# Attention scores as fp32 matmuls on the two row halves of the array, with unsplit q and k

## The chip, the cores and the metric

The kernel runs on one core of one Trainium2 chip. The metric is the device time of one execution in microseconds (us). A core has a matrix engine (PE, TensorE), a vector engine (DVE), an activation engine (ACT), a general engine (POOL, GpSimd) and a queue engine (SP) that issues the transfers (DMA). Matmuls write to PSUM, which has eight banks of 512 fp32 numbers per partition; everything else lives in SBUF, over 128 partitions.

## The reference, cut to what matters

Two layers of a hybrid encoder over 256 tokens, width 1024. Each layer normalises its input, applies one wide input projection, and feeds three branches: forgetting attention (16 heads of 64), a state-space scan, and differential attention (8 heads, each with two score matrices of 64 dims). The scores of the first and of the third are what the change touches:

```python
for i in range(L // Q_BLOCK):                                   # forgetting attention, Q_BLOCK = 128
    s = jnp.einsum('bhqd,bhkd->bhqk', q[:, :, q0:q1], k[:, :, :q1]).astype(jnp.float32) * scale
    s = s + F[:, :, q0:q1, None] - F[:, :, None, :q1]           # F: cumulative log forget gate
    p = jax.nn.softmax(jnp.where(tk <= tq, s, -jnp.inf), axis=-1).astype(v.dtype)
    outs.append(jnp.einsum('bhqk,bhkd->bhqd', p, v[:, :, :q1]))
...
for i in range(L // Q_BLOCK):                                   # differential attention, c = 0, 1
    s = jnp.einsum('bhcqd,bhckd->bhcqk', q[:, :, :, q0:q1], k[:, :, :, :q1]).astype(jnp.float32) * scale
    p = jax.nn.softmax(jnp.where(ck <= cq, s, -jnp.inf), axis=-1)
    a = (p[:, :, 0] - lam * p[:, :, 1]).astype(v.dtype)
    outs.append(jnp.einsum('bhqk,bhkd->bhqd', a, v[:, :, :q1]))
```

All inputs and outputs are fp32.

## The kernel before

**The projections.** Weights come from memory in units of 128x1024 (`raw`), and are split into a rounded part and a rest (`whi`, ACT, L231; `wlo`, DVE, L232) of the type fp32r, so that a product of three fp32r matmuls (hi·hi, hi·lo, lo·hi) has fp32 precision. `bform` (L249, 128x512 outputs) makes projections with tokens on the partitions, `aform` (L264, 128x256 outputs) makes those with features on the partitions. Together they are the main stream of PE work, in the order of `plan`. Everything else is written as generators (jobs); `pump` steps them between two projections, and the framework's scheduler then sets the final order on each engine by its own estimate of times. An engine works through its own list in that order.

**Scores before.** q and k have their features on the partitions: a tile of 128 partitions holds two heads (or the two halves of one differential head), one in partitions 0 to 63 and one in 64 to 127. `split_qk` builds from each tile new fp32r tiles: `stack_q` (L380, L381) puts the rounded half and its rest one above the other in 128 partitions, `stack_k` (L385 to L388) the rounded k twice, and its rest twice. `scores` then makes, for one head and one PSUM bank, four matmuls over all 128 rows of the array: 128 keys for the first 128 tokens and 256 keys for the next 128, each with k (L400) and with its rest (L401). DVE adds the bias and takes the maximum (L403), ACT takes the exponential (L406).

**The mask of forgetting attention.** `small_chain` makes the gates on DVE and then their running sums by matmuls (L359 to L366); DVE copies them out (`sc_cum`, L368, L369), SP writes them to memory (`scr`, L371) and reads them back spread over the partitions into the tile `sc` of each pair of heads (L422, L423); POOL masks two blocks of `sc` (L426). DVE's L403 reads `sc` as bias and writes the scores over it. Behind the softmax `sc` is transposed (L447) and multiplied by the values into `po` (L457), each head of a pair on one half of the array's columns.

**PSUM.** Three banks `pp` for the projections, three `pq` for scores, transposes of weights of attention and part of the scan, two `pt` for the other transposes, the scan's states and the products with the values.

Of the kernel before, what the change touches and what calls it, by code (L numbers as in the profile page):

```python
# [11 lines left out]
F32 = mybir.dt.float32  # L12
F32R = mybir.dt.float32r
AF = mybir.ActivationFunctionType
# [3 lines left out]
P = 128  # L18
# [78 lines left out]
def trunk(ctx: ExitStack, tc: tile.TileContext, x, norm_w, weights, small, vectors,  # L97
# [10 lines left out]
    sm = ctx.enter_context(tc.tile_pool(name="sm", bufs=2))  # L108
    dr = ctx.enter_context(tc.tile_pool(name="dr", bufs=1, space=bass.MemoryType.DRAM))
    pp = ctx.enter_context(tc.tile_pool(name="pp", bufs=3, space=bass.MemoryType.PSUM))  # L110
    pq = ctx.enter_context(tc.tile_pool(name="pq", bufs=3, space=bass.MemoryType.PSUM))
    pt = ctx.enter_context(tc.tile_pool(name="pt", bufs=2, space=bass.MemoryType.PSUM))

    SMALL = nc.sync

# [12 lines left out]
    def bank(pool, name):  # L128
        return pool.tile([P, 512], F32, name=name)
# [63 lines left out]
                                   op0=ALU.mult, op1=ALU.subtract)  # L193

    def split_rows(src, hi, lo, tt, c):
        ps = bank(pt, "pt")
        for j in range(4):
            PE.transpose(ps[:, j * P:(j + 1) * P], src[:, j * P:(j + 1) * P], ident)  # L198
        ts = slice(tt * P, (tt + 1) * P)
        p4 = ps.rearrange("p (i j t) -> p i j t", i=2, t=P)  # L200
        for i in range(2):
            last = split_bank(p4[:, i], hi[2 * c + i][:, :, ts], lo[2 * c + i][:, :, ts])
        return last
# [169 lines left out]

    SPANS = ((0, slice(0, P)), (1, slice(P, 384)))

    LOH, HIH = slice(0, 64), slice(64, P)

    def stack_q(src, dst):
        for q, main, rest in zip(dst, (LOH, HIH), (HIH, LOH)):
            S.copy(out=q[main], in_=src[main])  # L380
            V.tensor_tensor(out=q[rest], in0=src[main], in1=q[main].bitcast(F32), op=ALU.subtract)  # L381

    def stack_k(src, dst):
        for k, kl, main, rest in zip(dst[0:2], dst[2:4], (LOH, HIH), (HIH, LOH)):
            S.copy(out=k[main], in_=src[main])  # L385
            V.tensor_tensor(out=kl[main], in0=src[main], in1=k[main].bitcast(F32), op=ALU.subtract)
            S.copy(out=k[rest], in_=src[main])
            S.copy(out=kl[rest], in_=kl[main].bitcast(F32))  # L388

    def split_qk(key, src):  # L390
        tiles = [a2(dtype=F32R) for _ in range(2 if key[1] == "q" else 4)]
        (stack_q if key[1] == "q" else stack_k)(src, tiles)
        return tiles

    def scores(st, pre, b, i, sc, bias, nm, rs):
        j, tk = b % 2, st[f"{pre}k{b // 2}"]
        q, k, kl = st[f"{pre}q{b // 2}"][i], tk[i], tk[2 + i]
        ps = bank(pq, "pq")
        for o, qs, n in ((0, slice(0, P), P), (P, slice(P, T), T)):
            PE.matmul(ps[:, o:o + n], lhsT=q[:, j, qs], rhs=k[:, j, 0:n], start=True, stop=False)  # L400
            PE.matmul(ps[:, o:o + n], lhsT=q[:, j, qs], rhs=kl[:, j, 0:n], start=False, stop=True)  # L401
        for t, sl in SPANS:
            V.tensor_tensor_reduce(out=sc[:, sl], in0=ps[:, sl], in1=bias[:, sl], scale=-0.125, scalar=BIG,  # L403
                                   op0=ALU.add, op1=ALU.min, accum_out=nm[:, t:t + 1])
        for t, sl in SPANS:
            S.activation(out=sc[:, sl], in_=sc[:, sl], func=AF.Exp, scale=-1.0,  # L406
                         bias=nm[:, t:t + 1], accum_out=rs[:, t:t + 1])

    def fox(l):
        st = L[l]  # L410
# [5 lines left out]
    def fox_pair(l, b, yhi, ylo):  # L416
        st = L[l]
        hb, j = b // 2, b % 2
        yield from need(l, "scr")
        sc = sp.tile([P, 2, 384], F32, name="sc")  # L420
        rows = st["scr"][2 * b:2 * b + 2, :]
        SMALL.dma_start(sc[:, :, 0:P], rows[:, 0:P].partition_broadcast(P))  # L422
        SMALL.dma_start(sc[:, :, P:384], rows.partition_broadcast(P))  # L423
        for i in (0, 2):
            v = sc[:, :, i * P:(i + 1) * P]
            G.affine_select(out=v, in_=v, pattern=[[0, 2], [-1, P]], compare_op=ALU.is_ge,  # L426
                            fill=NEG, base=0, channel_multiplier=1)
        yield 1, 0.0
        yield from need(l, f"fq{hb}", f"fk{hb}")
        nm = sm.tile([P, 2, 2], F32, name="nm")  # L430
        rs = sm.tile([P, 2, 2], F32, name="rs")
        for i in range(2):
            scores(st, "f", b, i, sc[:, i, :], sc[:, i, :], nm[:, i, :], rs[:, i, :])
        ri = sm.tile([P, 2, 2], F32, name="ri")
        V.reciprocal(out=ri, in_=rs)
        V.tensor_scalar(out=ri, in0=ri, scalar1=0.5, scalar2=None, op0=ALU.mult)
        for i in range(2):
            for t, sl in SPANS:
                V.tensor_scalar(out=sc[:, i, sl], in0=sc[:, i, sl], scalar1=ri[:, i, t:t + 1],
                                scalar2=None, op0=ALU.mult)  # L440
        yield 2, 2.2
        yield from need(l, "fv", f"fg{hb}")
        pTs = []
        for i in range(2):
            ps = bank(pq, "pq")
            for t in range(3):
                PE.transpose(ps[:, t * P:(t + 1) * P], sc[:, i, t * P:(t + 1) * P], ident)  # L447
            pT = tp.tile([P, 384], F32, name="pT", bufs=3)
            done = S.copy(out=pT, in_=ps[:, 0:384]).ins
            pTs.append(pT)  # L450
        yield 1, 0.0
        po = bank(pt, "pt")
        with tc.high_priority(URGENT):
            for t, o, n in ((0, 0, T), (1, P, P)):
                for i in range(2):
                    h = 2 * b + i
                    mm = PE.matmul(po[64 * i:64 * i + 64, o:T],  # L457
                                   lhsT=st["fv"][t][h // 8][:, h % 8 * 64:(h % 8 + 1) * 64],
                                   rhs=pTs[i][:, t * T:t * T + n], start=(t == 0), stop=(t == 1))
                    if t + i == 0:  # L460
                        tc.add_manual_dep(mm.ins, done.name, mybir.DependencyInfo(
                            mybir.DependencyClass.Sync, mybir.DependencyReason.DATA), reason="both heads")
        yt = sc[:, 0, 0:T]
        V.tensor_tensor(out=yt, in0=po[:, 0:T], in1=st[f"fg{hb}"][:, j, :], op=ALU.mult)
        S.copy(out=at(yhi, b), in_=yt)
        V.tensor_tensor(out=at(ylo, b), in0=yt, in1=at(yhi, b).bitcast(F32), op=ALU.subtract)
        st["_yA"][1] += 1
        if st["_yA"][1] == 8:
            st["yA"] = st["_yA"][0]
        yield 1, 0.75  # L470
# [21 lines left out]
    def ssd_cb(l):  # L492
# [5 lines left out]
        for gp in range(2):  # L498
# [7 lines left out]
            V.tensor_tensor(out=m, in0=ps.rearrange("p (a b) -> p a b", b=P),  # L506
                            in1=upper.unsqueeze(1).broadcast_to([P, 4, P]), op=ALU.mult)
            cb.append(m)
        ps = bank(pt, "pt")
        for g in range(4):  # L510
            PE.transpose(ps[:, g * P:(g + 1) * P], bT[g // 2][:, g % 2, 0:P], ident)
        btok = sm.tile([P, 512], F32, name="btok", bufs=1)
# [6 lines left out]
    def ssd_x(l, c, tt):  # L519
# [7 lines left out]
        xdt, y = a2([P, 512]), a2([P, 512])  # L527
        st[f"xdt{tt}"].append(xdt)
        st[f"ys{tt}"].append(y)
        ps = bank(pt, "pt")  # L530
        for j in range(4):
            PE.transpose(ps[:, j * P:(j + 1) * P], xc[j // 2][:, j % 2, tt * P:(tt + 1) * P], ident)  # L532
        p3 = ps.rearrange("p (h d) -> p h d", d=64)
# [9 lines left out]
    def ssd_group(l, g):  # L543
# [33 lines left out]
                                   in1=st["cb"][c][:, 2 * (g % 2):2 * (g % 2) + 2, :].rearrange("p b k -> p (b k)")  # L577
                                   .unsqueeze(1).broadcast_to([P, 2, 256]), op=ALU.mult).ins
        yield 2, 3.2
        ps = bank(pt, "pt")  # L580
        PE.matmul(ps[:, 0:256], lhsT=st["btok"][:, g * P:(g + 1) * P], rhs=xdd[:, gs], start=True, stop=True)
        S.copy(out=st0[:, gs], in_=ps[:, 0:256])
        ps = bank(pq, "pq")
# [45 lines left out]
    def transposed(l, name, y, scale):  # L629
        yield 1  # L630
        yhi, ylo = halves()
        for j2 in range(4):
            ps = bank(pt, "pt")
            for i in range(2):
                j = 2 * j2 + i
                for tt in range(2):
                    PE.transpose(ps[:, i * T + tt * P:i * T + (tt + 1) * P], y[tt][j // 4][:, j % 4 * P:(j % 4 + 1) * P], ident)  # L637
            for i in range(2):
                j = 2 * j2 + i
                split_bank(ps[:, i * T:(i + 1) * T], at(yhi, j), at(ylo, j), scale(j))  # L640
            if j2 == 3:
                L[l][name] = (yhi, ylo)
            if j2 % 2:
                yield (1, 1.6)
# [3 lines left out]
    def rope(l, c):  # L648
# [16 lines left out]
        V.tensor_tensor(out=rp, in0=rp, in1=sw, op=ALU.add)  # L665
        for d_, s_ in views:
            SMALL.dma_start(s_, d_)
        yield 1, 2.4
        for key, src in (("dq", q), ("dk", k)):
            for jj in range(2):  # L670
                st[f"{key}{2 * c + jj}"] = split_qk(key, src[jj])
            yield 1, 1.2 if key[1] == "k" else 2.4

    def diff(l):
        L[l]["_d"] = 0
# [3 lines left out]
    def diff_head(l, h):  # L679
        st, pr = L[l], par[l]  # L680
        yield from need(l, f"dq{h // 2}", f"dk{h // 2}")
        sc = sp.tile([P, 2, 384], F32, name="sc")
        nm = sm.tile([P, 2, 2], F32, name="dnm")
        rs = sm.tile([P, 2, 2], F32, name="drs")
        for i in range(2):
            scores(st, "d", h, i, sc[:, i, :], bmask, nm[:, i, :], rs[:, i, :])
        ri = sm.tile([P, 2, 2], F32, name="dri")
        V.reciprocal(out=ri, in_=rs)
        V.tensor_scalar(out=ri[:, 1, :], in0=ri[:, 1, :], scalar1=pr["nlam"], scalar2=None, op0=ALU.mult)
# [37 lines left out]
    def plan(l):  # L727
# [38 lines left out]

        def t_evac(key):
            def f(jj, ps):
                st[f"{key[0:2]}{2 * int(key[2]) + jj}"] = split_qk(key, ps.rearrange("p (a t) -> p a t", t=T))
            return f  # L770

        def r_evac(key):
# [257 lines left out]
```

## Time and profile before

| | |
|---|---|
| time, median of 3 runs | 944.5 us (944.32 to 945.57) |
| profiled execution | 943.72 us, span of its instructions 942.0 us |
| PE busy | 928.9 us (99%), 6052 matmuls |
| DVE busy | 698.9 us (74%) |
| ACT busy | 598.0 us (63%) |
| POOL busy | 40.4 us (4%) |
| granted TensorE clock, mean | 0.994 |

Busy times are a share of the span. A matmul's record is longer than the room it takes in the stream, since the next one starts before it ends; the chain of work (which counts from one end to the next) is the view that gives a matmul's price in a full stream. An fp32 matmul has two records in the trace, an fp32r matmul one.

### The profile page before, as it was taken

How to read it: one execution, taken by the hardware profiler on the slowest of the kernel's cores; microseconds unless marked ns; L12 is line 12 of the kernel's file. 1: busy time of each engine (PE TensorE's matmuls, PEld its weight loads, DVE VectorE, ACT ScalarE, POOL GpSimd, SP SyncE). 2: the span in 40 equal slices, each digit the busy share in tenths (PEclk: the TensorE clock that was granted, in tenths of full speed). 3: DMA queues.
4: the chain of work that ended last, by engine and by line, in shares of the span. 5: the costliest groups of instructions: out<-in, count | busy, mean ns of one | idle time of the engine just before them, and what ended most of it. 6: DMA issues, size and time to landing. Idle time of an engine off the chain costs nothing.

```text
span 942.0 us, 16514 instructions
## 1 busy us (share of the span) xinstructions
PE 928.9 (99%) x6052; PEld 831.3 (88%) x6052; DVE 698.9 (74%) x1434; ACT 598.0 (63%) x1141; POOL 40.4 (4%) x71
## 2 busy tenths in 40 slices
PE   7999999999999999999999999999999999999997
PEld 6999999988898988888889999998889899888885
DVE  5778788989667877765758778789877677787473
ACT  5678786644567868554546869666545696885442
POOL 1002200000000000100000110000000000010000
PEclk7999999999999999999999999999999999999999
DMA  6866634674555655555558674456646456555551
GB/s 237 272 216 195 213 116 153 216 224 144 180 199 160 187 191 157 177 173 190 188 173 270 212 213 140 132 179 209 202 153 206 145 186 190 189 169 167 182 175 45
DMA packets 60320, 172.47 MB, mean 183 GB/s; under 512 B 7312, under 2 KB 15824, under 8 KB 60240
## 3 DMA queue, kind: packets, MB, share of 16 engines
q1 hardware_dynamic: 60240, 171.43, 55.8%
q8 instruction: 47, 0.77, 0.4%
q14 instruction: 33, 0.27, 0.1%
HBM read 167.14 MB, written 2.16 MB: 180 GB/s over the span
## 4 chain that ended last, share of the span: by engine, by line
PE 96%; DMA 2%; DVE 1%; ACT 0%; issue 0%; SPq 0%; POOL 0%; POOLq 0%
PE pp L249 51%; PE pp L264 33%; PE pq L400 2%; PE pq L401 1%; PE pt L457 1%; PE pq L447 1%; PE pq L590 1%; DMA raw<-in_weights_dram 1%; PE pt L637 1%; PE pt L198 1%; PE pq L702 1%; PE pq L600 0%; PE pt L532 0%; PE pt L710 0%; PE pq L503 0%; PE pt L709 0%
## 5 line engine op out<-in xcount | busy, mean ns | idle before, releaser
L249 PE MATMUL pp<-whi,a 128*128 128x512 f32 (+1 forms) x1472 | 451.6, 386 | 1.2 <-ACT whi L231 0.8
L232 DVE TENSOR_TENSOR wlo<-raw,whi 128x1024 fp32r<-128x1024 f32 (+1 forms) x296 | 349.6, 1193 | 79.4 <-ACT whi L231 76.3
L231 ACT CAST whi<-raw 128x1024 fp32r<-128x1024 f32 (+1 forms) x296 | 301.9, 1028 | 116.5 <-PE pp L249 68.3
L264 PE MATMUL pp<-a,whi 128*128 128x256 f32 x1792 | 332.4, 285 | 0.0
L249 PEld LDWEIGHTS pp<-whi,a 128*128 128x128 f32 x1472 | 272.9, 189 | 55.1 <-ACT whi L231 1.5
L264 PEld LDWEIGHTS pp<-a,whi 128*128 128x128 f32 x1792 | 281.2, 191 | 1.3 <-issue 1.0
L249 PE MATMUL pp<-wlo,a 128*128 128x512 f32 (+1 forms) x736 | 280.9, 384 | 0.0
L264 PE MATMUL pp<-a,wlo 128*128 128x256 f32 x896 | 254.4, 284 | 0.0
L264 PEld LDWEIGHTS pp<-a,wlo 128*128 128x128 f32 x896 | 171.5, 191 | 0.8 <-issue 0.8
L249 PEld LDWEIGHTS pp<-wlo,a 128*128 128x128 f32 x736 | 138.5, 189 | 25.8 <-DVE wlo L232 0.5
L183 POOL TENSOR_TENSOR rstd<-rstd,mhalf 128x2 f32<-128x2 f32 (+2 forms) x26 | 18.9, 727 | 740.0 <-DVE rstd L181 719.1
L477 DVE SCALAR_TENSOR_TENSOR a<-sw,pT,a 128x255 f32<-128x255 f32 (+2 forms) x96 | 42.0, 477 | 6.1 <-ACT a L474 6.0
L406 ACT ACTIVATE sc<-sc,dnm 128x128 f32<-128x128 f32 x64 | 28.6, 450 | 8.4 <-DVE dnm L403 8.3
L400 PE MATMUL pq<-a,a 128*128 128x128 f32 (+1 forms) x128 | 31.9, 284 | 0.4 <-DVE nm L403 0.4
L188 ACT CAST a<-pt 128x256 fp32r<-128x256 f32 x32 | 11.5, 371 | 32.6 <-PE pt L198 26.5
L819 DVE SCALAR_TENSOR_TENSOR a<-a,pp 128x512 f32<-128x512 f32 x24 | 16.4, 682 | 20.4 <-PE pp L249 20.4
L401 PE MATMUL pq<-a,a 128*128 128x128 f32 (+1 forms) x128 | 31.5, 269 | 0.0
L406 ACT ACTIVATE sc<-sc,nm 128x128 f32<-128x128 f32 (+1 forms) x64 | 28.5, 447 | 2.1 <-DVE nm L403 2.0
L426 POOL TENSOR_SCALAR_AFFINE_SELECT sc<-sc 128x256 f32<-128x256 f32 x32 | 19.7, 619 | 156.6 <-DMA sc<-scr 138.1
L400 PEld LDWEIGHTS pq<-a,a 128*128 128x128 f32 x128 | 23.7, 191 | 0.9 <-DVE nm L403 0.6
L403 DVE CUSTOM_DVE_ANT_0 sc<-pq,sc 128x128 f32<-128x128 f32 (+1 forms) x64 | 19.5, 351 | 6.6 <-POOL sc L426 5.6
L401 PEld LDWEIGHTS pq<-a,a 128*128 128x128 f32 x128 | 23.6, 191 | 0.3
(159 smaller groups left out, 807.7 us busy)
## 6 DMA issues: line engine op xcount, KB each, us to landing
raw<-in_weights_dram SPq DMA_DIRECT2D x280, 512.0 KB, 4.4
raw<-in_weights_dram SPq DMA_DIRECT2D x16, 272.0 KB, 3.3
sc<-scr SPq DMA_DIRECT2D x16, 256.0 KB, 5.5
a<-scr SPq DMA_DIRECT2D x16, 256.0 KB, 6.2
a<-in_x_dram SPq DMA_DIRECT2D x8, 256.0 KB, 5.3
sc<-scr SPq DMA_DIRECT2D x16, 128.0 KB, 5.0
a<-in_norm_w_dram SPq DMA_DIRECT2D x4, 256.0 KB, 6.5
rp<-a SPq DMA_DIRECT2D x32, 32.0 KB, 4.0
```

The costliest lines, as they stand in the source:

```text
L183: G.tensor_tensor(out=r[:, 0:width], in0=r[:, 0:width], in1=mhalf[:, 0:width], op=ALU.pow)
L231: S.copy(out=hi, in_=raw)
L232: V.tensor_tensor(out=lo, in0=raw, in1=hi.bitcast(F32), op=ALU.subtract)
L249: PE.matmul(ps[:, 0:n], lhsT=at(a, kt)[:, ts], rhs=w[:, k, 0:n], start=((u, k, i) == order[0]), stop=((u, k, i) == order[-1]))
L264: PE.matmul(ps[:, j * T:(j + 1) * T], lhsT=w[:, k, c0:c0 + P], rhs=at(a, kt), start=(kt == 0 and j == 0 and i == 0), stop=(kt == KT - 1 an ...
L400: PE.matmul(ps[:, o:o + n], lhsT=q[:, j, qs], rhs=k[:, j, 0:n], start=True, stop=False)
L401: PE.matmul(ps[:, o:o + n], lhsT=q[:, j, qs], rhs=kl[:, j, 0:n], start=False, stop=True)
L403: V.tensor_tensor_reduce(out=sc[:, sl], in0=ps[:, sl], in1=bias[:, sl], scale=-0.125, scalar=BIG, op0=ALU.add, op1=ALU.min, accum_out=nm[: ...
L406: S.activation(out=sc[:, sl], in_=sc[:, sl], func=AF.Exp, scale=-1.0, bias=nm[:, t:t + 1], accum_out=rs[:, t:t + 1])
L426: G.affine_select(out=v, in_=v, pattern=[[0, 2], [-1, P]], compare_op=ALU.is_ge, fill=NEG, base=0, channel_multiplier=1)
L477: V.scalar_tensor_tensor(out=xc[:, s:T], in0=u[:, 0:T - s], scalar=pr["conv"](j, k), in1=xc[:, s:T], op0=ALU.mult, op1=ALU.add)
L819: V.scalar_tensor_tensor(out=t, in0=t, scalar=1.0, in1=ps, op0=ALU.add, op1=ALU.mult)
```

## The change

Scores are made from q and k as they come out of the projection (for differential attention as `rope` leaves them), in fp32. The splitting functions are gone; `t_evac` copies a projection's bank to one fp32 tile. `scores` now takes both heads of a pair (or both halves of a differential head) and two banks: for 128 and for 256 keys it issues one matmul with partitions 0 to 63 of q and k and one with partitions 64 to 127, which lie on the upper and lower 64 rows of the array. The first of the four also waits for `held`, the instruction on POOL that last wrote `sc`: the second L426 of the pair for forgetting attention, a new one-column memset for differential attention. Four banks are `pq` and one is `pt`; all but the products with the values use `pq`. Some of `rope`'s yields change.

```diff
-    pq = ctx.enter_context(tc.tile_pool(name="pq", bufs=3, space=bass.MemoryType.PSUM))
-    pt = ctx.enter_context(tc.tile_pool(name="pt", bufs=2, space=bass.MemoryType.PSUM))
+    pq = ctx.enter_context(tc.tile_pool(name="pq", bufs=4, space=bass.MemoryType.PSUM))
+    pt = ctx.enter_context(tc.tile_pool(name="pt", bufs=1, space=bass.MemoryType.PSUM))
...
-    def stack_q(src, dst):
...
-    def stack_k(src, dst):
...
-    def split_qk(key, src):
...
-    def scores(st, pre, b, i, sc, bias, nm, rs):
-        j, tk = b % 2, st[f"{pre}k{b // 2}"]
-        q, k, kl = st[f"{pre}q{b // 2}"][i], tk[i], tk[2 + i]
-        ps = bank(pq, "pq")
+    def scores(st, pre, b, sc, bias, nm, rs, held):
+        j, q, k = b % 2, st[f"{pre}q{b // 2}"], st[f"{pre}k{b // 2}"]
+        ps = [bank(pq, "pq") for _ in range(2)]
         for o, qs, n in ((0, slice(0, P), P), (P, slice(P, T), T)):
-            PE.matmul(ps[:, o:o + n], lhsT=q[:, j, qs], rhs=k[:, j, 0:n], start=True, stop=False)
-            PE.matmul(ps[:, o:o + n], lhsT=q[:, j, qs], rhs=kl[:, j, 0:n], start=False, stop=True)
...
+            for i in range(2):
+                r = slice(64 * i, 64 * i + 64)
+                mm = PE.matmul(ps[i][:, o:o + n], lhsT=q[r, j, qs], rhs=k[r, j, 0:n], start=True, stop=True)
+                if o + i == 0:
+                    tc.add_manual_dep(mm.ins, held.name, mybir.DependencyInfo(
+                        mybir.DependencyClass.Sync, mybir.DependencyReason.DATA), reason="place for the scores")
...
-            G.affine_select(out=v, in_=v, pattern=[[0, 2], [-1, P]], compare_op=ALU.is_ge,
-                            fill=NEG, base=0, channel_multiplier=1)
+            held = G.affine_select(out=v, in_=v, pattern=[[0, 2], [-1, P]], compare_op=ALU.is_ge,
+                                   fill=NEG, base=0, channel_multiplier=1).ins
...
+        held = G.memset(sc[:, 0, 0:1], 0.0).ins
...
-                st[f"{key[0:2]}{2 * int(key[2]) + jj}"] = split_qk(key, ps.rearrange("p (a t) -> p a t", t=T))
+                t = a2()
+                S.copy(out=t, in_=ps.rearrange("p (a t) -> p a t", t=T))
+                st[f"{key[0:2]}{2 * int(key[2]) + jj}"] = t
```

The order moves with it. On PE in the first layer, from the last sum of the gates (L366) on, the kernel before goes on with 19 projection matmuls and the first scores (`a_615` is a q tile, `a_835` and `a_837` are k and its rest; the other L264 rows of this stretch read like the ones shown):

```order
L366 MATMUL pq<-ones,sc_l 16x128
L264 MATMUL pp<-a_150,wlo 128x256
...
L264 MATMUL pp<-a_151,wlo 128x256
L400 MATMUL pq<-a_835,a_615 128x128
L264 MATMUL pp<-a_152,whi 128x256
L264 MATMUL pp<-a_156,whi 128x256
L264 MATMUL pp<-a_152,wlo 128x256
L264 MATMUL pp<-a_152,whi 128x256
L401 MATMUL pq<-a_837,a_615 128x128
L400 MATMUL pq<-a_835,a_615 128x256
L401 MATMUL pq<-a_837,a_615 128x256
```

In the changed kernel 65 projection matmuls stand between L366 and the first scores (L382; `a2_827` is k, `a2_615` q, `pq_831` and `pq_832` are the banks of the two heads):

```order
L264 MATMUL pp_996<-a2_150,whi_550 128x256
L382 MATMUL pq_831<-a2_827,a2_615 128x128
L382 MATMUL pq_832<-a2_827,a2_615 128x128
L382 MATMUL pq_831<-a2_827,a2_615 128x256
L382 MATMUL pq_832<-a2_827,a2_615 128x256
```

So the first scores moved 46 projection matmuls further from L366, and the four of a pair stand together. The sums L359 to L366 themselves moved ahead by 21 projection matmuls. Two projection matmuls later the second pair follows, twelve later the third, and the fourth another two later; the third and fourth stand like this (`pq_928` and `pq_929` are the third pair's banks, `pq_951` and `pq_952` the fourth's):

```order
L382 MATMUL pq_928<-a2_924,a2_666 128x128
L382 MATMUL pq_928<-a2_924,a2_666 128x256
L382 MATMUL pq_929<-a2_924,a2_666 128x128
L382 MATMUL pq_929<-a2_924,a2_666 128x256
...
L382 MATMUL pq_951<-a2_924,a2_666 128x128
L382 MATMUL pq_951<-a2_924,a2_666 128x256
...
L382 MATMUL pq_952<-a2_924,a2_666 128x128
L382 MATMUL pq_952<-a2_924,a2_666 128x256
```

In these two pairs one head's matmuls stand ahead of the other's, and in the fourth a projection matmul stands between the heads. Elsewhere a pair's rows alternate between the heads, as in the fence before, except that in the last differential head of a layer one matmul stands apart. Per layer the 16 pairs stand in 14 uninterrupted stretches. The second layer has the same order.

On DVE, the copies of the running sums to SBUF stood like this before, in the first layer (L386 is one of the splits of k):

```order
L362 COPY sc_acs<-pq 128x32
L232 TENSOR_TENSOR wlo<-raw,whi 128x1024
L368 COPY sc_cum<-pq 32x256
L386 TENSOR_TENSOR a_838<-pp,a_836 64x512
L369 TENSOR_SCALAR sc_cum<-sc_cum 16x256
```

and stand like this in the changed kernel:

```order
L362 COPY sc_acs<-pq 128x32
L368 COPY sc_cum<-pq 32x256
L369 TENSOR_SCALAR sc_cum<-sc_cum 16x256
L232 TENSOR_TENSOR wlo<-raw,whi 128x1024
```

Nothing stands between the copies any more.

## Rows read from the trace of the kernel before

**Rows 1.** The page, part 1: busy us, share of the span, instructions.

```profile
PE 928.9 (99%) x6052; PEld 831.3 (88%) x6052; DVE 698.9 (74%) x1434; ACT 598.0 (63%) x1141; POOL 40.4 (4%) x71
```

**Rows 2.** Who PE waited for: us in total, times, longest us.

```profile
PE pt L198 <- DVE a L210: 2.6, 1, 2.6
PE pq L940 <- POOL mhalf L147: 2.0, 1, 2.0
PE pp L249 <- ACT whi L231: 0.8, 1, 0.8
PE pq L400 <- DVE nm L403: 0.4, 1, 0.4
```

**Rows 3.** The chain from 71.9 us: start us, us, what; one head's scores.

```profile
71.94 0.06 PE pq L400
...
72.40 0.60 PE pp L264 x5
```

**Rows 4.** The chain, 160 to 210 us: fp32 matmuls of 128 and 256 columns.

```profile
160.42 0.89 PE pq L503 x8
...
209.27 0.86 PE pt L581 x4
```

**Rows 5.** The chain from 86 us: products with the values, on column halves.

```profile
86.52 0.33 PE pq L447 x3
86.85 0.80 PE pt L457 x8
87.65 0.81 PE pq L447 x6
...
94.37 0.80 PE pt L457 x8
95.17 3.06 PE pp L264 x24
```

**Rows 6.** The chain from 59.9 us, in the first layer: last sum, projections.

```profile
59.98 0.22 PE pq L366 x2
60.20 2.46 PE pp L264 x19
```

**Rows 7.** DVE from 60 us, in order of time: start us, us, line.

```profile
60.70 0.41 DVE L368 COPY sc_cum<-pq 32x256 f32<-32x256 f32 x1
61.25 0.69 DVE L386 TENSOR_TENSOR a<-pp,a 64x512 fp32r<-64x512 f32 x1
61.97 0.28 DVE L369 TENSOR_SCALAR sc_cum<-sc_cum 16x256 f32<-16x256 f32 x1
```

**Rows 8.** POOL from 68 us, in order of time; idle before it in brackets.

```profile
69.60 0.41 POOL L426 TENSOR_SCALAR_AFFINE_SELECT sc<-sc 128x256 f32<-128x256 f32 x1 [0.28 <-DMA sc<-scr]
...
71.26 0.89 POOL L426 TENSOR_SCALAR_AFFINE_SELECT sc<-sc 128x256 f32<-128x256 f32 x2 [0.34 <-DMA sc<-scr]
```

**Rows 9.** The chain from 519 us, in the second layer: the mask's way.

```profile
519.81 0.22 PE pq L366 x2
...
522.12 3.54 DMA scr<-sc_cum
...
525.72 3.57 DMA sc<-scr
...
530.80 0.41 POOL sc L426
```

**Rows 10.** Groups by line on ACT and DVE: count, busy us, mean ns, idle before.

```profile
L388 ACT CAST a<-a 64x512 fp32r<-64x512 f32 x32 | 19.8, 619 | 0.6
L381 DVE TENSOR_TENSOR a<-pp,a 64x512 fp32r<-64x512 f32 x16 | 11.0, 689 | 0.9 <-ACT a L380 0.4
L403 DVE CUSTOM_DVE_ANT_0 sc<-pq,sc 128x128 f32<-128x128 f32 (+1 forms) x64 | 19.5, 351 | 6.6 <-POOL sc L426 5.6 <-PE pq L401 0.6
L464 DVE TENSOR_TENSOR sc<-pt,a 128x256 f32<-128x256 f32 x16 | 6.8, 422 | 7.5 <-PE pt L457 7.2
```

More of the change, by code (lines that the diff above doesn't have):

```diff
@@ L195, in split_rows @@
     def split_rows(src, hi, lo, tt, c):
-        ps = bank(pt, "pt")
+        ps = bank(pq, "pq")
         for j in range(4):
@@ L374, in trunk @@
     SPANS = ((0, slice(0, P)), (1, slice(P, 384)))
-    LOH, HIH = slice(0, 64), slice(64, P)
-    def stack_q(src, dst):
-        for q, main, rest in zip(dst, (LOH, HIH), (HIH, LOH)):
-            S.copy(out=q[main], in_=src[main])
-            V.tensor_tensor(out=q[rest], in0=src[main], in1=q[main].bitcast(F32), op=ALU.subtract)
-    def stack_k(src, dst):
[L384 to L388, printed above, removed]
@@ L390, in split_qk @@
-    def split_qk(key, src):
-        tiles = [a2(dtype=F32R) for _ in range(2 if key[1] == "q" else 4)]
-        (stack_q if key[1] == "q" else stack_k)(src, tiles)
-        return tiles
-    def scores(st, pre, b, i, sc, bias, nm, rs):
-        j, tk = b % 2, st[f"{pre}k{b // 2}"]
-        q, k, kl = st[f"{pre}q{b // 2}"][i], tk[i], tk[2 + i]
-        ps = bank(pq, "pq")
-        for o, qs, n in ((0, slice(0, P), P), (P, slice(P, T), T)):
-            PE.matmul(ps[:, o:o + n], lhsT=q[:, j, qs], rhs=k[:, j, 0:n], start=True, stop=False)
-            PE.matmul(ps[:, o:o + n], lhsT=q[:, j, qs], rhs=kl[:, j, 0:n], start=False, stop=True)
[L402 to L407, printed above, removed]
+    def scores(st, pre, b, sc, bias, nm, rs, held):
+        j, q, k = b % 2, st[f"{pre}q{b // 2}"], st[f"{pre}k{b // 2}"]
+        ps = [bank(pq, "pq") for _ in range(2)]
+        for o, qs, n in ((0, slice(0, P), P), (P, slice(P, T), T)):
+            for i in range(2):
[4 more added lines that the diff above has]
+                        mybir.DependencyClass.Sync, mybir.DependencyReason.DATA), reason="place for the scores")
+        for i in range(2):
+            for t, sl in SPANS:
+                V.tensor_tensor_reduce(out=sc[:, i, sl], in0=ps[i][:, sl], in1=bias(i)[:, sl], scale=-0.125,
+                                       scalar=BIG, op0=ALU.add, op1=ALU.min, accum_out=nm[:, i, t:t + 1])
+            for t, sl in SPANS:
+                S.activation(out=sc[:, i, sl], in_=sc[:, i, sl], func=AF.Exp, scale=-1.0,
+                             bias=nm[:, i, t:t + 1], accum_out=rs[:, i, t:t + 1])
@@ L431, in fox_pair @@
         rs = sm.tile([P, 2, 2], F32, name="rs")
-        for i in range(2):
-            scores(st, "f", b, i, sc[:, i, :], sc[:, i, :], nm[:, i, :], rs[:, i, :])
+        scores(st, "f", b, sc, lambda i: sc[:, i, :], nm, rs, held)
         ri = sm.tile([P, 2, 2], F32, name="ri")
@@ L508, in ssd_cb @@
             cb.append(m)
-        ps = bank(pt, "pt")
+        ps = bank(pq, "pq")
         for g in range(4):
@@ L529, in ssd_x @@
         st[f"ys{tt}"].append(y)
-        ps = bank(pt, "pt")
+        ps = bank(pq, "pq")
         for j in range(4):
@@ L579, in ssd_group @@
         yield 2, 3.2
-        ps = bank(pt, "pt")
+        ps = bank(pq, "pq")
         PE.matmul(ps[:, 0:256], lhsT=st["btok"][:, g * P:(g + 1) * P], rhs=xdd[:, gs], start=True, stop=True)
@@ L632, in transposed @@
         for j2 in range(4):
-            ps = bank(pt, "pt")
+            ps = bank(pq, "pq")
             for i in range(2):
@@ L667, in rope @@
             SMALL.dma_start(s_, d_)
-        yield 1, 2.4
+        yield 2, 2.4
         for key, src in (("dq", q), ("dk", k)):
             for jj in range(2):
-                st[f"{key}{2 * c + jj}"] = split_qk(key, src[jj])
-            yield 1, 1.2 if key[1] == "k" else 2.4
+                st[f"{key}{2 * c + jj}"] = src[jj]
+        yield 1, 0.0
     def diff(l):
@@ L682, in diff_head @@
         sc = sp.tile([P, 2, 384], F32, name="sc")
+        held = G.memset(sc[:, 0, 0:1], 0.0).ins
         nm = sm.tile([P, 2, 2], F32, name="dnm")
         rs = sm.tile([P, 2, 2], F32, name="drs")
-        for i in range(2):
-            scores(st, "d", h, i, sc[:, i, :], bmask, nm[:, i, :], rs[:, i, :])
+        scores(st, "d", h, sc, lambda i: bmask, nm, rs, held)
         ri = sm.tile([P, 2, 2], F32, name="dri")
```

## The prediction, made before the changed kernel had run

> **What bounds the kernel now.** I read the page's busy shares first: PE is busy 99% of the span [rows 1]. Since a busy PE may still wait inside a record, the list of whom PE waited for comes next: 2.6, 2.0 and 0.8 us belong to the start (first transposes, warm-up, first weights), and in the hundreds of us behind it there is one wait of 0.4 us, at the scores [rows 2]. So PE's stream is the bound, and the price of an edit is what it does to that stream, read from the chain of work, which counts from one end to the next. What ACT and DVE save is worth nothing unless PE waits for it later: the change takes some 128 casts of about 0.62 us off ACT and 64 subtractions of about 0.69 us off DVE [rows 10], 79 and 44 us, and gives ACT 16 copies; but PE waits for neither. That work is covered by the stream of projections.
>
> **What the scores cost before.** One head runs from 71.94 to 72.40 us: 0.46 us [rows 3]. 64 heads (16 per layer and branch): 29.4 us.
>
> **What they cost in fp32.** An fp32 matmul has two records. Of 128 columns, eight records take 0.89 us, 0.11 us each; of 256 columns, four take 0.86 us, 0.215 us each [rows 4]. A pair of heads now has four records of each size, 1.30 us if they run one after another on the array. The trace has no matmul on row halves. The nearest is L457, on column halves, with just these eight records: its piece takes 0.80 us [rows 5]. That is 0.65 us for two halves at the same time, plus 0.15. The bounds of a pair's stream are therefore 0.65 and 1.30 us; I take 0.65, as the form nearest by count, type and size does it: 32 x 0.65 = 20.8 us.
>
> **What changing the array's form costs.** The 0.15 us ahead of L457 is one side. Behind it, six transposes take 0.81 us where three take 0.33 us, so 0.15 more; 24 projection matmuls take 3.06 us, where 0.60 us for five [rows 3] would give 2.88, so 0.18 more [rows 5]. In and out is about 0.31 us. It falls on each uninterrupted stretch of scores, of which the new order has 14 per layer: 28 x 0.31 = 8.7 us. The bounds are 0 (row halves might switch freely) and 8.7; I take 8.7, since the only measured switch paid it both ways.
>
> **Where halves don't stand side by side.** In the third and fourth pair of each layer one head stands ahead of the other. The fourth has a projection matmul between them and loses the whole overlap, 0.65 us; the third lies between 0 and 0.44 us lost (one record of 0.215 can still overlap at the seam), I take 0.22; the last differential head has its two 256-column matmuls apart, 0.43. That is 1.3 us per layer, 2.6 in all; bounds 1.0 and 3.0, the lower if PE looks past a whole head.
>
> So the scores go from 29.4 to 20.8 + 8.7 + 2.6 = 32.1 us: **+2.7 us**.
>
> **The wait for the mask.** Before, L403 on DVE waited for POOL's mask (5.6 us in all [rows 10]), while PE went on. Now the first score matmul of a pair waits itself, and behind it on PE stands everything, projections above all. How late is the mask? In the first layer L366 ends at 60.20 us [rows 6], the first pair's second mask ends at 70.01 us [rows 8]: 9.8 us. In the second layer it is 520.03 to 531.21 us, 11.2 us; the write to memory takes 3.54 us there and the read 3.57 us and more [rows 9]. What the change shortens is DVE's part: L369 ended at 62.25 us, 2.05 us behind L366 [rows 6, 7], with a 0.69 us subtraction and the end of a weight split in between. With L368 (0.41) and L369 (0.28) alone it would be 0.8 us, so the mask comes 1.25 us sooner: 8.55 and 9.95 us behind L366. PE has 65 projection matmuls for that, 65 x 0.12 = 7.8 us. It waits 0.75 us in the first layer and 2.15 us in the second. In the first layer the second pair's mask ends 1.66 us behind the first's (71.67 against 70.01 [rows 8]); PE comes to it after a pair (0.65), the switch (0.31) and two projection matmuls (0.24), 1.2 us, and waits 0.45 us more. Together **3.35 us**. The bounds: nothing, if both transfers together land 2.15 us faster than they did in the second layer; 6.15 us, if they are slower in each layer by another 1.4 us, by which the layers differ. I take the measured latencies. The 0.4 us that PE waited before at L400 [rows 2] goes.
>
> **What costs nothing.** That L359 comes 21 projection matmuls earlier (2.5 us) is paid for by the four subtractions that left DVE's queue ahead of it (4 x 0.69 = 2.8 us). The third pair needs the first's banks back: DVE takes four L403 for that, 1.4 us [rows 10], and PE is 2.4 us away. The single bank `pt` is asked for again after 24 projection matmuls at least, 2.9 us, and freed in the first branch by one 0.42 us instruction [rows 10]; if the longer release in the third branch is late, each time costs some tenths, for which the range has room. SP's queue keeps its order but for two weight loads that now stand behind the ten mask reads; their units are needed some 20 us later. The new memsets on POOL (4% busy [rows 1]) wait for a free `sc`, as DVE did.
>
> **The sum.** +2.7 + 3.35 - 0.4 = +5.65 us. On the profiled execution's 943.72 us (span 942.0) it gives 949.4 us; on the median of the runs, 0.8 us above it, **950.1 us**.
>
> [...] The column halves of L457 take 0.80 us for what is 1.30 us in a row [rows 5, 4]; two records that follow each other in the program on one half have let those of the other half pass. [...]
>
> **The rivals.**
> 1. *The row halves run one after another.* A pair costs 1.30 us. For: no row of the trace shows row halves together. Against: the column halves. 32 pairs take 41.6 us, against 20.8 + 2.6: 950.1 + 18.2 = 968 us. Chance 0.10.
> 2. *Strict order with overlap at the seams only.* A record of one half then overlaps only the last one of the other half ahead of it. For a pair that is 0.11 + 0.11 + 0.11 + 0.105 + 0.215 + 0.215 = 0.865 us, 27.7 us for 32 pairs, and 1.3 us more for the heads that stand apart: 29.0 against 23.4, +5.6 and 955.7 us. Against: the same order would give L457 1.0 us, and it took 0.80. Chance 0.08.
> 3. *Row halves switch without the 0.31 us* (ends on the faster side). [...] It makes the kernel faster by over 0.2% (about what a measurement of this kernel can tell from no change; 1.9 us) once 0.27 of the 0.31 us is gone at each stretch, the waits for the mask staying. For: the measured switch is one of columns. Against: both of its sides paid, also the one back to the full array. Chance 0.11.
> 4. *The masks come in time.* The scheduler put 65 matmuls there by its own estimate; if the transfers land by 2 us sooner now that fewer weight loads stand among them, the 3.35 us goes: 946.8 us, and 945.2 if the heads that stand apart cost 1.0 and not 2.6 us. Against: the mask was late for L403 in both layers. Chance 0.13, a little over half of it within 0.2%.
>
> **How the numbers follow.** My forecast has 0.58; its own range, from the bounds of the mask (0 to 6.15) and of the order (1.0 to 3.0), is 945 to 953.5 us. A range of 942 to 957.5 us leaves out the first rival (0.10) and most of the third (0.09). Faster: the third rival and a little of the fourth, 0.13. Within 0.2% (942.6 to 946.4): most of the fourth and the low end of the forecast, 0.12. Slower: 0.75.
>
> **What would show it.** In the chain after, a stretch of one pair (eight records of L382) of 0.80 us, one of two pairs of 1.45, and the projection piece behind it 0.15 to 0.18 us over 0.12 us a matmul; 1.45 us for one pair would be the first rival, 1.0 the second, 0.65 the third. In the list of PE's waits a new line, PE at L382 for POOL's mask, of 2.5 to 4 us in about three times, the largest in the second layer; without it the fourth rival is right. ACT should be some 70 us and DVE some 40 us less busy, with PE's count of records unchanged at 6052. The prediction is wrong if PE waits at other places, above all for the single bank `pt` or for a memset on POOL.

## The result, and the profile after

| | before | after |
|---|---|---|
| median of 5 runs | 944.5 us (943.86 to 945.57) | 953.13 us (952.68 to 953.57) |
| profiled execution, span | 943.72, 942.0 us | 952.68, 950.6 us |
| mean granted TensorE clock | 0.994 | 0.997 |

The ratio is 1.0092, with a 95% interval of 1.0082 to 1.0103: slower by 8.6 us, where 5.6 were forecast.

The page after, part 1 (compare [rows 1]):

```profile
PE 932.2 (98%) x6052; PEld 819.1 (86%) x6052; DVE 660.4 (69%) x1370; ACT 532.0 (56%) x1029; POOL 41.3 (4%) x87
```

ACT is 66 us less busy and DVE 38.5, with the same 6052 records on PE. None of the 104 us shows in the time, because PE's stream is still the bound. Whom PE waited for (us in total, times, longest), against [rows 2]:

```profile
PE pq L198 <- DVE a L210: 3.2, 2, 2.5
PE pp L249 <- ACT a L748: 2.1, 2, 1.1
PE pq L926 <- POOL mhalf L147: 2.0, 1, 2.0
PE pp L249 <- ACT a L188: 1.9, 2, 1.2
PE pq L382 <- POOL sc L411: 1.3, 2, 1.0
PE pp L249 <- ACT whi L231: 0.8, 1, 0.8
```

L198, L926, L188 and L231 belong to the first 25 us; L188 had 0.4 us before. Behind the start two waits are new. One was forecast, L382 for the mask. The other was not: the projections (L249) for L748, the tanh that copies a finished mixing-gate projection out of its bank.

The chain of work in the first layer, from the second pair of scores on (start us, us, what; compare [rows 3]):

```profile
68.08 0.93 PE pq L382 x8
69.01 1.63 PE pp L264 x12
70.64 0.86 PE pq L382 x8
71.50 0.43 PE pp L264 x2
71.93 0.85 PE pq L382 x4
72.78 0.32 PE pp L264
73.09 0.85 PE pq L382 x4
73.94 2.34 PE pp L264 x18
...
108.92 1.51 PE pq L382 x16
110.43 1.63 PE pp L264 x12
```

Read the pieces against each other. A stretch of two pairs (x16) takes 1.51 us and one of a single pair (x8) 0.86. The second pair adds 0.65 us, which is the price that the prediction gave to two halves side by side, and 0.86 - 0.65 = 0.21 us is the way in. Behind a stretch 12 projections take 1.63 us where 12 x 0.12 = 1.44 would do, and two take 0.43 for 0.24: 0.19 us is the way out. In the trace the records of the stretch at 108.9 us start in twos, 7 ns apart. The third pair (70.64), whose heads stand one after the other, costs 0.86 us like the others; its four records of 128 columns start first, in twos 13 to 14 ns apart, and then its four of 256 (70.57 to 70.79 us, then 70.89 to 71.12), though in the program one head's 256 columns stand ahead of the other's 128. The fourth, with a projection between its heads, costs 0.85 twice: one head alone takes as long as a pair.

The mask's way in the second layer (compare [rows 9]):

```profile
522.21 0.42 DVE sc_cum L368
...
522.66 0.29 DVE sc_cum L369
...
522.97 1.65 DMA scr<-sc_cum
...
524.68 3.59 DMA sc<-scr
...
528.42 1.28 POOL sc L411
...
530.10 1.04 POOL sc L411
...
531.19 0.93 PE pq L382 x8
```

DVE's part is 0.75 us behind L366, as forecast (0.8). The write to memory took 1.65 us here and 3.54 us before, and the first of the pair's two masks starts 6.2 us behind L366, where it was 9.4 before. But the masks themselves took 1.28 and 1.04 us here, and 0.41 us each at this place in the kernel before. DVE in the same stretch:

```profile
528.21 1.23 DVE L232 TENSOR_TENSOR wlo<-raw,whi 128x1024 fp32r<-128x1024 f32 x1 [0.22 <-ACT whi L231]
529.64 1.23 DVE L232 TENSOR_TENSOR wlo<-raw,whi 128x1024 fp32r<-128x1024 f32 x1 [0.21 <-ACT whi L231]
```

Each of the two masks runs beside a weight split on DVE and ends 0.27 us behind the end of that split (529.44 and 530.87). So do all seven masks of this profile that take more than 0.5 us (0.55 to 1.44 us); the other 25 take 0.40 to 0.41. In the kernel before DVE had no split to do while it waited there for these masks.

Now the wait that was not forecast. ACT in order of time, near the end of the first layer (start us, us, line; idle before it in brackets), then PE in the same stretch:

```profile
427.09 0.47 ACT L191 ACTIVATE a<-pq,pT 128x256 fp32r<-128x256 f32 x1 [4.64 <-PE pq L621]
427.46 1.56 ACT L748 ACTIVATE a<-pp 128x512 f32<-128x512 f32 x3
```

```profile
426.68 0.38 PE L621 MATMUL pq<-ident,a 128*128 128x128 f32 x2
428.11 0.50 PE L249 MATMUL pp<-whi,a 128*128 128x512 f32 x1 [1.05 <-ACT a L748]
```

L191 splits one bank of the third branch's transposes. It stands in ACT's order ahead of three L748 and is idle for 4.64 us, until PE comes to the last two L621 of that bank. The copies run on ACT behind it, from 427.46 us on, and behind the L621 the next group of projections wants a bank of `pp` that the first copy frees. PE is idle for 1.05 us; from the end of L621 (427.06) to the end of the next matmul (428.61) it is 1.55 us, where 0.23 is usual, so 1.32 us are lost, and the same in the second layer. Before, PE waited for no such copy.

### The profile page after: what moved, and what is told of

The parts are those of the page before. It is cut to its first block, busy times and chain, and to the rows that moved or that the text cites. A ratio compares the mean times of both kernels' runs of the same rounds, so it can differ in the third digit from the quotient of the medians.

```text
span 950.6 us, 16315 instructions
## 1 busy us (share of the span) xinstructions
PE 932.2 (98%) x6052; PEld 819.1 (86%) x6052; DVE 660.4 (69%) x1370; ACT 532.0 (56%) x1029; POOL 41.3 (4%) x87
## 4 chain that ended last, share of the span: by engine, by line
PE 91%; issue 6%; DMA 1%; POOL 1%; DVE 0%; ACT 0%; POOLq 0%; SPq 0%; DVEq 0%
PE pp L249 49%; PE pp L264 31%; PE pq L382 3%; PE pt L441 1%; PE pq L431 1%; PE pq L574 1%; PE pq L621 1%; PE pq L686 1%; PE pq L198 1%; POOL sc L411 0%; PE pt L692 0%; PE pq L584 0%; DMA sc<-scr 0%; PE pt L694 0%; PE pq L487 0%
## 5 line engine op out<-in xcount | busy, mean ns | idle before, releaser
L249 PE MATMUL pp<-whi,a 128*128 128x512 f32 (+1 forms) x1472 | 449.5, 386 | 4.9 <-ACT a L748 2.1
L232 DVE TENSOR_TENSOR wlo<-raw,whi 128x1024 fp32r<-128x1024 f32 (+1 forms) x296 | 350.7, 1196 | 100.5 <-ACT whi L231 95.8
L231 ACT CAST whi<-raw 128x1024 fp32r<-128x1024 f32 (+1 forms) x296 | 302.2, 1028 | 129.6 <-PE pp L249 68.4
L264 PE MATMUL pp<-a,whi 128*128 128x256 f32 x1792 | 329.7, 285 | 0.0
L249 PEld LDWEIGHTS pp<-whi,a 128*128 128x128 f32 x1472 | 271.4, 188 | 58.4 <-ACT a L748 3.1
L264 PEld LDWEIGHTS pp<-a,whi 128*128 128x128 f32 x1792 | 279.7, 192 | 5.9 <-issue 5.0
L249 PE MATMUL pp<-wlo,a 128*128 128x512 f32 (+1 forms) x736 | 281.5, 384 | 0.1
L264 PE MATMUL pp<-a,wlo 128*128 128x256 f32 x896 | 255.0, 285 | 0.0
L264 PEld LDWEIGHTS pp<-a,wlo 128*128 128x128 f32 x896 | 171.6, 191 | 2.4 <-issue 2.4
L249 PEld LDWEIGHTS pp<-wlo,a 128*128 128x128 f32 x736 | 138.1, 188 | 27.8 <-issue 1.3
L391 ACT ACTIVATE sc<-sc,nm 128x128 f32<-128x128 f32 x64 | 28.3, 443 | 11.2 <-DVE nm L388 10.0
L382 PE MATMUL pq<-a,a 64*128 64x256 f32 (+1 forms) x256 | 30.7, 344 | 1.3 <-POOL sc L411 1.3
L192 DVE SCALAR_TENSOR_TENSOR a<-pq,pT,a 128x256 fp32r<-128x256 f32 x32 | 14.7, 480 | 23.5 <-ACT a L191 23.0
L188 ACT CAST a<-pq 128x256 fp32r<-128x256 f32 x32 | 11.4, 370 | 32.6 <-PE pq L198 26.0
L191 ACT ACTIVATE a<-pq,pT 128x256 fp32r<-128x256 f32 x32 | 14.6, 476 | 20.6 <-PE pq L621 17.7
L382 PEld LDWEIGHTS pq<-a,a 64*128 64x128 f32 x256 | 19.1, 186 | 7.7 <-issue 3.5
L388 DVE CUSTOM_DVE_ANT_0 sc<-pq,bmask 128x128 f32<-128x128 f32 x64 | 19.0, 353 | 9.3 <-PE pq L382 9.3
L433 ACT COPY pT<-pq 128x384 f32<-128x384 f32 x32 | 13.9, 481 | 18.5 <-PE pt L441 18.5
```

Of the source, the lines that this page charges most:

```text
L191: S.activation(out=hi, in_=ps, func=AF.Copy, scale=scale)
L192: V.scalar_tensor_tensor(out=lo, in0=ps, scalar=scale, in1=hi.bitcast(F32), op0=ALU.mult, op1=ALU.subtract)
L231: S.copy(out=hi, in_=raw)
L232: V.tensor_tensor(out=lo, in0=raw, in1=hi.bitcast(F32), op=ALU.subtract)
L249: PE.matmul(ps[:, 0:n], lhsT=at(a, kt)[:, ts], rhs=w[:, k, 0:n], start=((u, k, i) == order[0]), stop=((u, k, i) == order[-1]))
L264: PE.matmul(ps[:, j * T:(j + 1) * T], lhsT=w[:, k, c0:c0 + P], rhs=at(a, kt), start=(kt == 0 and j == 0 and i == 0), stop=(kt == KT - 1 an ...
```

## The experiments

Times are medians; the kernel before ran on the same chip each time, and gave 943.9 to 944.5 us. "Scores in all" below is worked out from the trace: the score records from one end to the next, without waits, and what the record behind each stretch took beyond the usual of its kind. It is 34.1 us for the changed kernel in 28 stretches. For the kernel before the same reckoning gives 29.9 us, where the prediction had 29.4.

**The scores not held behind the mask.**

```diff
-                if o + i == 0:
-                    tc.add_manual_dep(mm.ins, held.name, ...
...
-        held = G.memset(sc[:, 0, 0:1], 0.0).ins
```

> The changed kernel without the wait of the first score matmul for POOL (held), and without the one-column memset. In its order the pairs then stand in 20 stretches of row halves in place of 28, and the first scores stand 30 projection matmuls behind L366 in place of 65, in four banks at once. Theory (the loss is 0.9 us at the start, 2.6 us where PE waits for ACT's tanh of the merge gates, 1.2 us at the mask, and about 4 us from the array's change of form at 0.40 us a stretch): the wait for the mask goes (1.85 us) and 8 stretches less save 3.2 us: 948 us; PE still waits twice for the tanh. Rival (held costs little and the banks carry the loss): 952 us, with PE waiting for PSUM banks behind the first eight score matmuls.

Measured: 948.11 us (946.92 to 949.35), ratio 1.0042 [1.0029, 1.0056]. The wait for the mask is gone, and the scheduler now makes 20 stretches instead of 28; scores in all take 30.3 us. That is 3.8 us for the stretches and 1.4 us for the wait in the profiled run, for 5.0 measured. The two come off together, so this run alone doesn't part them. The waits for the tanh copy stay (2.1 us, 2).

**The kernel before with the new banks alone.**

```diff
-    pq = ... bufs=3
-    pt = ... bufs=2
+    pq = ... bufs=4
+    pt = ... bufs=1
...
-        ps = bank(pt, "pt")
+        ps = bank(pq, "pq")
```

The last edit stands at the five places of transposes and scan.

> The kernel before (split q and k, full array) with the new PSUM pools alone: four banks for scores, transposes and scan, one for the products with the values. In its order, too, the last transposes of the third branch stand apart, with a split on ACT ahead of three tanh of the merge gates. Theory: PE waits for the tanh once in each layer, 1.3 us each, and nothing else changes: 947 us. Rival (the whole loss is the price of row halves): 944.5 us. Rival (the banks carry most of the loss): 950 us or more.

Measured: 955.33 us (953.89 to 957.94), ratio 1.012 [1.0104, 1.0137]: my theory failed, and by its time the rival held that wanted 950 us or more. Whom PE waited for, behind the start:

```profile
PE pq L637 <- DVE a L717: 4.4, 2, 2.2
...
PE pp L249 <- ACT a L764: 2.1, 2, 1.1
```

With one bank for value products, the last head's passes through PE, ACT, DVE, POOL and DVE again (L717) while the third branch's transposes (L637) stand next on PE. The tanh copy (L764 here) is late behind them, as in the changed kernel. The loss then grows. Busy times by stretch, with the granted clock (PEclk) behind POOL's:

```profile
core 0: us, PE busy (x) PEld busy (x) DVE busy (x) ACT busy (x) POOL busy (x), PEclk, DMA share, GB/s
420.00:428.60 8.60, 5.37 (x27) 4.14 (x26) 1.77 (x6) 2.98 (x9) 0.70 (x1) 1.00 0.29 93
428.60:432.00 3.40, 3.40 (x9) 2.65 (x9) 1.71 (x2) 1.19 (x3) 0.00 (x0) 0.50 0.00 0
```

PE was busy for 5.37 of 8.60 us, and behind that its clock was granted at half (0.50) for 3.4 us: 9 records, where 3.4 us hold 15 at the 0.227 us that a record of L249 takes in the chain from 419.94 us on (12 in 2.72). So the tanh wait belongs to the banks, and the order that comes with them, and not to the row halves. Most of this run's loss, the wait for L717 and the clock, is not in the changed kernel: the run does not show that the banks carry most of the loss there.

**The changed kernel with the banks as before** (the same edit backwards).

> The changed kernel with the old PSUM pools (three and two banks, transposes and scan states back in the pool of two). With three banks for scores, a pair's second head often has no bank: 18 stretches per layer in place of 14, and six pairs' worth of heads per layer without a partner beside them. Theory: the two waits for the tanh go (-2.6 us), eight more stretches cost 3.2 us and twelve lost overlaps 0.65 us each, 7.8 us: 961 us. Rival (the banks carry the loss): 947 us or less.

Measured: 959.37 us (957.95 to 963.0), ratio 1.0166 [1.0147, 1.0185]. The wait for the tanh copy shrinks to 0.8 us, once. But with three banks in `pq` only one pair and a half fit, and the scheduler sets heads apart:

```profile
67.20 0.93 PE pq L382 x8
68.13 0.43 PE pp L264 x2
68.56 0.85 PE pq L382 x4
69.41 3.52 PE pp L264 x16
```

36 stretches, many with a head alone (x4) at a pair's price: scores in all 42.9 us, 8.8 more than in the changed kernel. The last row of the fence holds a second loss: 16 projections take 3.52 us, 0.22 each where 0.12 is usual. They come soon behind a wait of 1.0 us for the mask (ahead of the first row; the list of PE's waits has 2.1 us in two), and beyond 16 x 0.12 and a way out of 0.19 us they cost some 1.4 us; what made them slow isn't shown. With 1.6 us less for the tanh copies, 0.8 more for the masks and 0.4 less at the start it makes 9.0 us, for 8.8 by which the spans of the two profiled executions differ. The execution that was profiled took 963.0 us; the medians are 6.2 us apart. The theory (961 us) came close and the rival (947 us or less) is refuted: the four banks are worth more here than the tanh wait that they bring.

**The changed kernel once more**, a single run with a profile.

> The changed kernel once more, for its start: up to the first 128x256 projection matmul it took 40.5 us where the kernel before took 39.6, with the same order of instructions. If the 0.9 us are the kernel's, this profile has 40.5 again; if they are chance, it may lie anywhere between 39.6 and 40.5.

Measured: 953.58 us. The list of PE's waits has

```profile
PE pq L382 <- POOL sc L411: 2.7, 3, 1.0
```

against 1.3, 2 in the first profile, with the same order of instructions. The mask's lateness differs from run to run; 2.7 us in three waits is close to the forecast. The tanh waits are the same 2.1 us. The first 128x256 projection begins at 40.0 us here, so of the 0.9 us that the expectation asks about 0.5 didn't come back.

**The third branch's transposes started later.**

```diff
     def transposed(l, name, y, scale):
         yield 1
+        if name == "yC":
+            yield from need(l, "mg21")
```

They start only when the copies of the last mixing-gate projections stand in the order.

> The changed kernel (953.1 us), with the third branch's transposes and their splits started only when the tanh copies of the last mixing-gate projections have been put in ScalarE's order, so that no split stands ahead of three of these copies. Theory (the wait of the projections for the tanh copy, 1.32 us in each layer, is part of the loss): 950.5 us, and the page shows no wait of TensorE for that copy. Rival (the wait only used up slack that a later wait would have used, or the later splits make the last product of the third branch wait): 953 us or more.

Measured: 950.24 us (949.79 to 950.72), ratio 1.0066 [1.0053, 1.0078]; 2.9 us less than the changed kernel. ACT at the same place:

```profile
425.81 0.60 ACT L750 ACTIVATE a<-pp 128x512 f32<-128x512 f32 x1 [3.96 <-PE pp L249]
426.30 0.86 ACT L191 ACTIVATE a<-pq,pT 128x256 fp32r<-128x256 f32 x2
```

The copy now comes ahead of the split, and the list of PE's waits has no line for it. The waits for the mask are 2.5 us in this profile.

**Both waits taken away**: this edit on the kernel with the scores not held.

> The same later splits, and the score products no longer held behind the mask (948.1 us with that alone). Theory (both waits are separate terms and add up): 948.1 - 2.6 = 945.5 us, which leaves the row halves about 1 us above the kernel before. Rival (the two losses share one cause, or the splits make a later product wait): 948 us or more.

Measured: 945.5 us (944.8 to 946.36, 11 runs), ratio 1.0015 [1.0006, 1.0024], to the tenth what the theory gave. The tanh waits are a term of their own, worth 2.6 us here and 2.9 above.

**Both heads of a pair on one row half.**

```diff
-                r = slice(64 * i, 64 * i + 64)
+                r = slice(0, 64)
```

> The changed kernel with both score products of a pair on the lower row half (q and k of the first head or map used twice, so the second's scores are left out and the first's stand in their place). Same number, shapes and order of instructions. Theory (the two halves stream side by side: a pair takes 0.65 us, not 1.30): 32 pairs x 0.65 = 20.8 us more, 974 us. Rival (the halves ran one after the other before, and 0.65 us was a cheaper product): no difference, 953 us.

Measured: 973.2 us (972.04 to 975.78), ratio 1.0312 [1.0297, 1.0328]; 20.1 us more than the changed kernel, for 20.8 expected. The expectation counted 2.1 us too much, since the heads that stand apart had no overlap to lose: the theory gives 18.7 us. In the trace scores in all take 52.8 us, 18.7 more, and the spans of the two profiled executions differ by 19.4 us, 0.8 of it a longer wait for the masks. The third pair in the chain:

```profile
72.66 1.50 PE pq L382 x8
74.16 0.43 PE pp L264 x2
```

1.50 us, where the two halves took 0.86; the way out is still 0.19. What overlaps is the two halves and not just two small matmuls.

**More stretches with the same products**, on the version without both waits.

```diff
                 mm = PE.matmul(ps[i][:, o:o + n], ...)
+                behind(mm, tr)
...
+            if o == 0:
+                tr = PE.transpose(ps[1][:, 384:512], ident, ident)
+                for m in pair:
+                    behind(tr, m)
```

`behind` sets the order on PE.

> The version without both waits (945.5 us), with a full-array transpose of the identity, written beside the scores and never read, between the two column parts of every head: 32 transposes of 0.11 us, and 56 stretches of row-half products instead of 20. Theory (a stretch costs 0.40 us beyond its products, 0.21 on the way in and 0.19 on the way out): 945.5 + 36 x 0.40 + 32 x 0.11 = 963.4 us. Prediction's price of 0.31: 960.2 us. Rival (no price on a change of form): 945.5 + 3.5 = 949 us.

Measured: 962.96 us (962.52 to 963.39), ratio 1.0198 [1.0182, 1.0214]: 17.5 us more than without the transposes, for 17.9 expected. The first stretches in the chain:

```profile
62.62 0.42 PE pq L388 x4
63.04 0.26 PE pq L393
63.30 0.85 PE pq L388 x8
64.16 0.26 PE pq L393
64.42 0.63 PE pq L388 x4
65.05 1.03 PE pp L264 x7
```

A transpose of 0.11 us (three in 0.33, [rows 5]) takes 0.26 between scores, 0.15 more, and each group of scores takes 0.2 us more than its stream (0.22 us for four records of 128 columns, 0.43 for four of 256). In and out is 0.35 us around a transpose, and 0.40 around projections. The price belongs to the stretch and not to the number of products in it: it is 0.20 us beyond the stream for four records and for eight.

**Fewer stretches.** The last four differential heads are taken in twos; their four banks are touched first by DVE, so that no score starts before all are free.

```diff
+        touch = [V.memset(ps[h][i][:, 0:1], 0.0) for h in range(len(heads)) for i in range(2)]
...
+                    if first is None:
+                        for v in touch:
+                            tc.add_manual_dep(mm.ins, v.ins.name, ...)
...
+        if h % 2 == 0 and h >= LATE:
+            st["_dps"] = score_products(st, "d", (h, h + 1))
```

> The version without both waits (945.5 us), with the last four heads of the difference attention taken two at a time: their four banks are touched by VectorE first and the products of both heads stand together, so that a layer has 8 stretches of row-half products instead of 10. Theory (0.40 us for a stretch): 945.5 - 4 x 0.40 = 943.9 us, the time of the kernel before. Rival (the wait for the fourth bank stands on TensorE and takes back as much, or more): 945.5 us or more.

Measured: 942.54 us (941.49 to 943.85, 11 runs), ratio 0.9982 [0.9973, 0.9991]: faster than both kernels, than the kernel before by 1.9 us. These heads in the chain, in the version without both waits and then here:

```profile
355.99 1.50 PE pq L382 x12
...
360.92 0.86 PE pq L382 x8
...
363.59 0.85 PE pq L382 x4
...
373.79 0.86 PE pq L382 x8
```

```profile
361.36 1.51 PE pq L392 x16
362.87 0.42 PE pt L719 x2
...
369.67 1.51 PE pq L392 x16
371.18 1.58 PE pp L250 x6
```

4.07 us become 3.02, and two ways out of 0.19 go: 1.43 us in a layer, 2.9 in both, for 3.0 measured. I had expected 1.6, since I had counted the four stretches and forgotten the head that stood apart (x12 and x4), which costs 0.63 us. No wait for the touched banks is in the list of PE's waits; it has one of 0.3 us at a score of the first branch, for a copy on ACT.

## Why the prediction was right, and where it was not

**The bound.** Right. PE's stream decides: 104 us less work on ACT and DVE gave nothing, and each edit above cost or gained what it did to PE's stream or its waits.

**The stream of a pair, 20.8 us.** Right: 0.65 us for a pair in the chain, and with both heads on one half 1.50 us with the way in, 20.1 us more for the whole. The first rival (halves in a row) is refuted. The second (strict order, overlap at the seams alone) wanted 0.865 us for a pair and falls too: 0.65 on row halves, and a third pair that loses nothing, with one head's records ahead of records of the other that stand earlier in the program.

**The array's form, 28 x 0.31 = 8.7 us.** The mechanism was right and the size too small: 0.21 + 0.19 = 0.40 us, 28 x 0.40 = 11.2 us, 2.5 us more. The 0.31 was read from column halves [rows 5], as 0.15 in and a mean of 0.15 and 0.18 out. The way out is the same for both: behind the fourth pair 18 projections take 2.34 us, 0.18 over 0.12 each, like the 24 behind L457, and a transpose behind scores costs 0.15 more. Most stretches stand ahead of projections, so the mean was a little low. The way in differs, 0.21 us in place of 0.15. It is the form that costs, and not fp32 beside fp32r: in the kernel before eight fp32 records on the full array take 0.11 us each [rows 4], and the 40 projections behind them 0.12 each:

```profile
161.32 4.79 PE pp L264 x40
```

The third rival (a free switch) is refuted by the run with 56 stretches: 17.5 us where it gave 3.5. The change has a price, 0.40 us for a stretch; no row shows what the array does meanwhile.

**The heads that stand apart, 2.6 us.** Nearly right. The fourth pair lost 0.63 us (0.65 forecast), the last differential head 0.41 (0.43), the third pair nothing (0.22): 2.1 us for both layers. So the scores came to 20.8 + 11.2 + 2.1 = 34.1 us, where the prediction had 32.1. Against 29.9 us before that is +4.2 us in place of +2.7.

**The wait for the mask, 3.35 us.** Right in kind and place, and too high for the profiled execution, where it cost 1.4 us beyond the way in (0.3 and 1.1). In the second profile it cost 2.9 us. The prediction looked to the transfers for what moves it. They landed sooner in the second layer, and POOL's masks took back part of that, held up beside DVE's weight splits: with 0.41 us for the last of them the first pair could have started 0.6 us sooner there, an estimate from the two rows of L411 and L232. That hold-up is in no term of the prediction, so the size of the wait owes something to luck.

**"What costs nothing."** This is the step that failed. By the prediction's own sign (PE waits at other places) it was wrong here. I followed the single bank `pt`, and allowed some tenths for a late release in the third branch. The cost came from the other side: with the transposes in `pq`, ACT got a split ahead of three tanh copies, and PE waited for those copies through `pp`, a pool that the change doesn't touch. It is 2.6 us, shown by its absence in the two runs with the later transposes.

**The sum.** +4.2 for the scores, +2.6 for the tanh copies, +1.4 - 0.4 for the masks, and 0.9 us at the start, where the first projection of 256 columns begins at 40.5 us instead of 39.6: 8.7 us, for 8.6 between the spans of the two profiled executions. Whether a part of the 0.9 belongs to the change isn't shown: the nine profiles with scores on row halves have this projection at 39.1 to 40.8 us, eight of them later than the one profile of the kernel before. The forecast of 950.1 us was 3 us low: 1.5 in the scores, 2.6 in the missed wait and the 0.9 at the start, against 1.9 too much for the mask. It came as close as it did because these errors went against each other.

## What to carry to other kernels

Count the stretches, not only the products: scores as half-height products side by side gained 29.9 - 20.8 = 9.1 us of stream here, and 28 stretches with their 0.40 us for the array's change of form took all of it back; with 16 stretches and the two waits gone the same change is 0.2% faster than before. When tiles move to another pool, read on each engine what now stands ahead of the copies that free the other pools' banks, since the wait showed there (2.1 us in two). And a product that another one parted from its partner cost as much as the pair, 0.85 us against 0.86.

## What was not expected of the hardware

Entering row halves costs 0.21 us, more than the 0.15 us read for column halves [rows 5]; leaving them costs 0.19 us beside projections and 0.15 us beside transposes, like column halves. An fp32 head alone on one half (x4, 0.85 us) costs as much as a pair (x8, 0.86). In the third pair's stretch PE started records of one half ahead of records of the other that stand earlier in the program: its last record of 128 columns at 70.79 us, its first of 256 at 70.89. A mask that started on POOL while DVE was at a weight split ended 0.27 us behind the split, in all seven cases of the first profile of the changed kernel: up to 1.44 us in place of 0.41. And waits can cost more than their length: in the kernel before with the new banks, PE's granted clock stood at 0.50 for 3.4 us behind a stretch in which it had been busy for 5.37 of 8.60 us. The half clock didn't follow each wait: in the first profile of the changed kernel PE waited three times for 1.04 or 1.05 us behind the start, and the clock stood at 1.00 from 15.7 to 947.0 us.
